# The layer-0 MLP's first product by one level of Strassen (seven half products for eight), with residual and gates resting in DRAM

## The chip, the core and the metric

The kernel runs on one core of a Trainium2 chip. A core has a matrix engine (TensorE, PE in the profile; PEld is its weight load), a vector engine (VectorE, DVE), a scalar engine (ScalarE, ACT), GpSimd (POOL) and SyncE (SP), which here issues the transfers between the chip's DRAM and the core's on-chip memory (SBUF). Each engine takes its own queue of instructions in order; they wait for each other by semaphores. TensorE adds its products up in PSUM, from where DVE or ACT must take them.

The metric is the device time of one execution in microseconds (us), as the median of several runs. Before the change it is 1242.63 us.

## The reference

Two layers of a diffusion transformer over 512 latent and 256 context tokens of width D = 1024. Layer 0 mixes tokens by pooling, layer 1 by attention. Each layer has a squared-ReLU MLP after its mixer, and each sub-layer is wrapped in RMS norms with shift, scale and gate that come from a linear map of the conditioning ("adaLN").

```
def sq_relu_mlp(h, w_in, w_out):
    return jnp.square(jax.nn.relu(h @ w_in)) @ w_out

for i in range(DEPTH):
    sh1, sc1, gt1, sh2, sc2, gt2 = ada_mods(c, w_ada[i], b_ada[i])
...
    x = x + gt1 * rms_norm(y_lat, g_mix_post[i])
    m_lat = sq_relu_mlp(modulate(rms_norm(x, g_mlp_pre[i]), sh2, sc2), w_mlp_in[i], w_mlp_out[i])
    x = x + gt2 * rms_norm(m_lat, g_mlp_post[i])
```

The context goes the same way through layer 0, with its own conditioning. `w_in` is 1024 x 4096, `w_out` 4096 x 1024, `w_ada` 1024 x 6144 per layer, all in float32.

## The kernel before

Precision: every float32 factor is split into a high part (a copy rounded to the matrix engine's fp32r form) and a low part (factor minus high), and each product is three matmuls: high by high, high by low, low by high. A weight block is thus loaded raw (1 MB, 128 partitions x 2048 columns) and split by a cast on ACT (L112) and a subtraction on DVE (L115), 2048 columns each. `Ring.load` does this: the raw block goes to one of three rotating buffers (pool `rawp`), the split halves to the next of three 4096-column units. The adaLN weights pass through the same three raw buffers.

The layer-0 MLP (`mlp`, from L580) works on all 768 tokens at once, in 16 groups of 256 hidden units. For a group:

- `w_out` of this group and `w_in` of the next are loaded and split into units.
- `Inner` (the class at L495) makes the first product of the next group: 2 blocks of 128 hidden units x 8 contraction blocks x 3 matmuls x 2 chunks of 384 tokens, 96 matmuls (L510) into PSUM. `square` takes them out: Relu (L518) and Square to the high part (L520) on ACT, r*r (L521) and its low part (L522) on DVE, 768 columns each.
- `out_mm` makes the second product of this group: 6 token tiles x 12 matmuls of 512 columns (L597), and `out_ev` adds each half tile to the running sum `acc` on DVE (L608), 12 additions of 128 x 512.

The first product of a group runs ahead of the second product of the one before it. Groups 14 and 15 are joined in one last second product.

DVE has a second task in the groups: `ada_sum` computes later adaLN vectors directly, without TensorE. For a 1 MB block of `w_ada` it makes one scaling (L238) and seven multiply-adds (L243) of 256 columns for each conditioning vector, a transpose (L246) and a reduction (L248). `extra0` starts one such block per group with two conditioning vectors (16 wide steps) while any are left and with one after that; `mid0` one with a single vector (8 steps). Their results are collected a group later (`ada_fin`, L211 and L221 in the profile). In group 6 `gate_diag` builds the MLP's gate rows.

Before the groups lies the prologue (the pool mixer, the first adaLN vectors on TensorE (L204), the norms, and the first product of group 0), whose steps have times written by hand (`Steps`). `residual` (L302) there updates the residual stream `xr` tile by tile. After the groups, `before0` and `last0` finish the last second product, add the residual, and start layer 1.

The order of instructions on each queue comes from a scheduler that simulates the program when it is built, except for those pinned by `keep_in_program_order` (the adaLN scalings, and all loads and splits up to group 1). Loads are issued from SyncE's queue (L98) in order; an issue waits until the last reader of the raw buffer that it takes is through.

Of the kernel before, what the change touches and what calls it, by code (L numbers as in the profile page):

```python
# [53 lines left out]
def backbone(ctx: ExitStack, tc, x, c, ctx_in, c_ctx, w_ada, b_ada, g_mix_pre, g_mix_post,  # L54
# [7 lines left out]
    rawp = ctx.enter_context(tc.tile_pool(name="rawp", bufs=3, side="right"))  # L62
    tmp = ctx.enter_context(tc.tile_pool(name="tmp", bufs=3, side="right"))
    psA = ctx.enter_context(tc.tile_pool(name="psA", bufs=2, space=PSUM))
    psB = ctx.enter_context(tc.tile_pool(name="psB", bufs=4, space=PSUM))

    xr = const.tile([P, NT, D], F32, name="xr")
    acc = const.tile([P, NT * D], F32, name="acc")
    gate = const.tile([P, 2, D], F32, name="gate")
    ident = const.tile([P, P], F32, name="ident")  # L70
# [6 lines left out]
    nhalf = const.tile([P, 4], F32, name="nhalf")  # L77
    junk = const.tile([P, D], BF16, name="junk")
# [3 lines left out]
    phase = ctx.enter_context(tc.tile_pool(name="phase", bufs=1)).tile([P, 40], F32, name="phase")  # L82
    rawe = ExitStack()
# [223 lines left out]

    def modulated_pair(t, i, s, hi, lo, works, wide, fine, on_act):
        ci = 0 if t < NL else 1
        sh = (SH1, SH2)[s] * KT  # L310
        sl = slice(t * P, (t + 2) * P)
        pss = []
# [12 lines left out]
        for q in range(4):  # L325
            h = works[q // 2][:, 512 * (q % 2):512 * (q % 2) + 512].rearrange("p (k n) -> p k n", n=256)
            for kk in range(2):
                k = 2 * q + kk
                sa, b = avec[i][s][:, k, ci:ci + 1], mods[i][:, sh + k, ci:ci + 1]
                if not on_act[k]:  # L330
                    ve.tensor_scalar(out=h[:, kk, :], in0=pss[q][:, kk, :], scalar1=sa, scalar2=b,
                                     op0=ALU.mult, op1=ALU.add)
                else:
                    sc.activation(h[:, kk, :], pss[q][:, kk, :], AF.Identity, scale=sa, bias=b)
            if fine:
                ks = slice(2 * q, 2 * q + 2)
                sc.copy(hi[:, ks, sl], h)  # L337
                ve.tensor_tensor(out=lo[:, ks, sl], in0=h, in1=hi[:, ks, sl], op=ALU.subtract)
            elif q % 2:
                ks = slice(2 * q - 2, 2 * q + 2)  # L340
                h = works[q // 2].rearrange("p (k n) -> p k n", n=256)
                sc.copy(hi[:, ks, sl], h)
                ve.tensor_tensor(out=lo[:, ks, sl], in0=h, in1=hi[:, ks, sl], op=ALU.subtract)

# [137 lines left out]
    def chunks0(g):  # L482
        if g == 0:
            return [[(1, 0, 512, 256)], [(0, 0, 0, 256)], [(0, 256, 256, 256)]], [(0, 1, 512, 0), (1, 1, 256, 512)]
        return [[(0, 0, 0, 384), (1, 0, 384, 384)]], [(0, 2, 384, 0)]
# [9 lines left out]
    class Inner:  # L495
# [6 lines left out]
        def part(self, c, f):  # L502
            (wH, wL), (aH, aL) = self.w, self.a
            if f not in self.ps:
                self.ps[f] = psA.tile([P, 2, 512], F32, tag="a", name="psin")
            ps, fs = self.ps[f], slice(f * P, (f + 1) * P)
            for k in range(KT):
                for n, (w, a) in enumerate(((wH, aH), (wH, aL), (wL, aH))):
                    for bank, o, t0, ln in self.chunks[c]:
                        te.matmul(ps[:, bank, o:o + ln], w[:, k, fs], a[:, k, t0:t0 + ln],  # L510
                                  start=(k == 0 and n == 0), stop=(k == KT - 1 and n == 2))

        def square(self, f):
            hi, lo = self.hid
            r = work_tile()[:, 0:self.ntok]
            q = work_tile()[:, 0:self.ntok]
            for b0, nb, ln, t0 in self.pieces:
                sc.activation(r[:, t0:t0 + nb * ln].rearrange("p (b n) -> p b n", n=ln),  # L518
                              self.ps[f][:, b0:b0 + nb, 0:ln], AF.Relu)
# [11 lines left out]

    ring = Ring(unit)

    def w_in(i, g, rg, pin=False, wait=None):
# [30 lines left out]
    for n, t in enumerate(order):  # L565
# [14 lines left out]
    def mlp(i, inner, rg, hids, order, extra, mid, last, before_last):  # L580
# [6 lines left out]
        def out_mm(parts, t, cols=HALVES):  # L587
            ts_ = slice(t * P, (t + 1) * P)
            pss = [psB.tile([P, 512], F32, tag="b", name="pso") for _ in cols]
# [19 lines left out]

        wo_, wi = w_out(i, 0, rg, True), w_in(i, 1, rg, True)  # L610
        for f in range(2):
            if len(inner.chunks) > 1:
                inner.part(len(inner.chunks) - 1, f)
            inner.square(f)
        for g in range(NG - 1):
            if g:
                wo_, wi = w_out(i, g, rg, g < 2), w_in(i, g + 1, rg, g < 2)
            part = (g, inner.hid, wo_)
            if g == NG - 2:
                wo_ = w_out(i, NG - 1, rg)  # L620
            extra(g)
            inner = Inner(g + 1, wi, aH, aL, hids[(g + 1) % len(hids)], CHUNKS[ntok], ntok)
            inner.run((lambda: mid(g)) if g < NG - 2 else None)
            if g < NG - 2:
                for t in range(tiles):
# [31 lines left out]
    def extra0(g):  # L657
# [7 lines left out]
        if g == 2:  # L665
            sc.activation(junk[:, 0:1], nhalf[:, 0:1], AF.Exp)
        if g == 6:
            gate_diag(0, GT2, 0)
            gate_diag(0, GT2, 1)

# [161 lines left out]

    def before0():
        qring.append(Ring([unit[0], unit[2], unit[1]]))
        w_chunk(2, 0, raw0)
# [7 lines left out]
    pTL = unit[1][:, 0:NT * LAT].rearrange("p (s n) -> p s n", n=LAT)  # L843
    pbuf = [xr[:, 4, 0:TOK], xr[:, 5, 0:TOK], gate[:, 1, 0:TOK], acc[:, 4 * D:4 * D + TOK]]
    aring = Ring([ra[:, 8192:12288], unit[0], unit[1], unit[2]])
# [16 lines left out]
    def s_scores(i):  # L862
# [5 lines left out]
        for n, (a, b) in enumerate(((qH, kTH), (qH, kTL), (qL, kTH))):  # L868
            for c2 in range(2):
# [4 lines left out]
        ve.tensor_reduce(out=sm[:, 0:1], in_=v, axis=AX.XY, op=ALU.max, negate=True)  # L874
        sc.activation(pbuf[i % 4].rearrange("p (c n) -> p c n", n=384), v, AF.Exp, bias=sm[:, 0:1],
                      accum_out=sm[:, 1:2])
        smx[i] = sm

    def s_norm(i):
        sm, p = smx[i], pbuf[i % 4]  # L880
        ve.reciprocal(sm[:, 2:3], sm[:, 1:2])
# [5 lines left out]
    def s_turn(i):  # L887
        _, t = steps[i]
        sl = slice(t * P, (t + 1) * P)
        p = pbuf[i % 4]  # L890
        for b in range(2):
# [171 lines left out]
```

## Time and profile before

| what | us |
|---|---|
| median of 3 runs (lowest, highest) | 1242.63 (1242.49, 1243.06) |
| the profiled execution, its own time | 1242.43 |
| its span, first to last instruction | 1240.4 |
| from the end of group 0's second product to the first product of group 15 | 446.43 |
| one group in it | 33.52 |

The profiled execution's time and its span differ by 2.0 us that lie around the instructions. The granted TensorE clock is 0.994 of full speed on average.

How its rows read: a row of grouped instructions gives line, engine, operation, output and inputs, shapes and a count, then the busy time in us, the mean in ns, and the idle time before it with what ended it. A row of the chain gives start and duration in us, then the engine and line that the end waited for. A row of the timeline gives start, busy time, engine, line and operation, with idle time in brackets. A row of windows gives the stretch, its length, then the busy time and count of PE, PEld, DVE, ACT and POOL, the granted clock, the busy share of the DMA engines and GB/s. A row of DMA issues gives the count, the size and the time from issue to landing. Where instructions follow each other without a gap, the step from start to start is shorter than the busy time of one, since the ends overlap; the steps are the price.

### The profile page before, as it was taken

The page shows a single profiled execution, that of the slowest core. Times are in us where ns is not written, and L with a number is a line of the kernel's source. Part 1 is how long each engine was busy: PE and PEld are TensorE (multiplying, and loading weights), DVE is VectorE, ACT ScalarE, POOL GpSimd, SP SyncE. Part 2 cuts the span into 40 slices and gives each one's busy share as a digit, 9 for nine tenths or more (in the row PEclk, how much of TensorE's full clock was granted, in tenths as well). Part 3 has the DMA queues.
Part 4 walks back from the last instruction along what each step waited for, and adds up shares of the span by engine and source line. Part 5 has one row for each costly group of instructions (what it writes and reads, how often), then busy time and mean ns, then how long its engine had stood idle before and what let it go on. Part 6 is the DMA issues. An engine that isn't in the chain of part 4 may idle for free.

```text
span 1240.4 us, 16687 instructions
## 1 busy us (share of the span) xinstructions
PE 1197.7 (97%) x6770; PEld 1043.0 (84%) x6770; DVE 868.1 (70%) x1424; ACT 452.5 (36%) x734; POOL 102.0 (8%) x135
## 2 busy tenths in 40 slices
PE   6799999999999999999999989999999999999997
PEld 5579889999888888899978869998878888888886
DVE  3788887788887877766387689972665564555555
ACT  5575122122212121222267357862633222313222
POOL 1061000000000000000152232001100000000001
PEclk9999999999999999999999999999999999999999
DMA  9991434444323344335121211011134232332201
GB/s 330 349 306 69 130 109 136 136 137 136 123 82 107 131 136 136 117 122 170 35 85 52 103 35 35 1 39 65 48 122 137 68 122 83 102 102 84 86 1 68
DMA packets 103276, 137.41 MB, mean 111 GB/s; under 512 B 2416, under 2 KB 87840, under 8 KB 103200
## 3 DMA queue, kind: packets, MB, share of 16 engines
q1 hardware_dynamic: 103200, 136.35, 33.8%
q8 instruction: 53, 0.87, 0.3%
q14 instruction: 23, 0.19, 0.0%
HBM read 134.24 MB, written 2.10 MB: 110 GB/s over the span
## 4 chain that ended last, share of the span: by engine, by line
PE 84%; DVE 5%; issue 3%; DMA 3%; ACT 3%; POOL 2%; SPq 0%; POOLq 0%; DVEq 0%; ACTq 0%
PE psin L510 35%; PE pso L597 34%; PE psy L935 3%; PE po L909 3%; PE psq L703 3%; PE pss L870 2%; PE pspool L442 2%; PE pspt L895 1%; DMA raw<-in_w_pool 1%; DMA raw<-in_w_ada 1%; ACT junk L138 1%; PE psada L204 1%; DVE xr L302 1%; DMA xr<-in_x 1%; DVE work L299 1%
## 5 line engine op out<-in xcount | busy, mean ns | idle before, releaser
L597 PE MATMUL pso<-units,rb 128*128 128x512 f32 (+1 forms) x1182 | 278.9, 391 | 1.7 <-DVE units L115 1.2
L608 DVE TENSOR_TENSOR acc<-acc,pso 128x512 f32<-128x512 f32 (+1 forms) x281 | 183.5, 680 | 125.5 <-PE pso L597 125.5
L597 PEld LDWEIGHTS pso<-units,rb 128*128 128x128 f32 x1182 | 220.5, 188 | 47.4 <-DVE units L115 1.6
L510 PE MATMUL psin<-ra,units 128*128 128x384 f32 (+1 forms) x1184 | 240.3, 345 | 0.9 <-ACT units L112 0.9
L510 PEld LDWEIGHTS psin<-ra,units 128*128 128x128 f32 x1184 | 209.1, 188 | 11.8 <-ACT units L112 1.7
L112 ACT CAST units<-raw 128x2048 fp32r<-128x2048 f32 (+1 forms) x50 | 80.1, 1623 | 263.4 <-PE pso L597 155.5
L243 DVE SCALAR_TENSOR_TENSOR rows<-raw,cond,rows 128x256 f32<-128x256 f32 x280 | 119.9, 478 | 0.2
L510 PE MATMUL psin<-ra,rb 128*128 128x384 f32 (+1 forms) x688 | 115.7, 320 | 2.8 <-ACT ra L337 1.6
L510 PEld LDWEIGHTS psin<-ra,rb 128*128 128x128 f32 x688 | 111.4, 189 | 4.2 <-ACT ra L337 2.0
L115 DVE TENSOR_TENSOR units<-raw,units 128x2048 fp32r<-128x2048 f32 (+1 forms) x48 | 95.3, 1998 | 24.8 <-ACT units L112 24.8
L518 ACT ACTIVATE work<-psin 128x512 f32<-128x512 f32 (+1 forms) x66 | 45.0, 685 | 178.2 <-PE psin L510 171.5
L521 DVE TENSOR_TENSOR work<-work 128x768 f32<-128x768 f32 (+1 forms) x64 | 52.6, 822 | 78.8 <-ACT work L518 78.5
L597 PE MATMUL pso<-ra,rb 128*128 128x512 f32 (+1 forms) x390 | 91.0, 386 | 0.0
L149 POOL TENSOR_SCALAR ms<-ss 128x1 f32<-128x1 f32 x21 | 8.8, 418 | 965.9 <-ACT junk L138 964.9
L597 PE MATMUL pso<-rb 128*128 128x512 f32 x360 | 85.3, 392 | 0.1
L597 PEld LDWEIGHTS pso<-ra,rb 128*128 128x128 f32 x390 | 72.5, 188 | 15.1 <-ACT rb L520 0.4
L510 PE MATMUL psin<-ra 128*128 128x512 f32 x256 | 80.2, 389 | 0.0
L597 PEld LDWEIGHTS pso<-rb 128*128 128x128 f32 x360 | 67.1, 188 | 13.8 <-DVE acc L606 0.4
L112 ACT CAST ra<-raw 128x2048 fp32r<-128x2048 f32 x16 | 30.4, 1908 | 105.4 <-PE pso L597 79.7
L510 PEld LDWEIGHTS psin<-ra 128*128 128x128 f32 x256 | 48.0, 188 | 10.0
L522 DVE TENSOR_TENSOR rb<-work,rb 128x768 fp32r<-128x768 f32 (+1 forms) x64 | 52.2, 815 | 3.0
L115 DVE TENSOR_TENSOR ra<-raw,ra 128x2048 fp32r<-128x2048 f32 x16 | 36.6, 2292 | 24.0 <-ACT ra L112 24.0
(174 smaller groups left out, 1582.9 us busy)
## 6 DMA issues: line engine op xcount, KB each, us to landing
raw<-in_w_ada SPq DMA_DIRECT2D x48, 1024.0 KB, 7.9
raw<-in_w_mlp_in SPq DMA_DIRECT2D x32, 1024.0 KB, 5.5
raw<-in_w_mlp_out SPq DMA_DIRECT2D x32, 1024.0 KB, 5.0
raw<-in_w_qkv SPq DMA_DIRECT2D x6, 1024.0 KB, 5.3
raw<-in_w_o SPq DMA_DIRECT2D x4, 1024.0 KB, 5.6
xr<-in_x SPq DMA_DIRECT2D x4, 512.0 KB, 4.7
out<-xr SPq DMA_DIRECT2D x8, 256.0 KB, 2.0
xr<-in_ctx SPq DMA_DIRECT2D x2, 512.0 KB, 5.6
```

What stands on the lines that cost most here:

```text
L112: a = gp.tensor_copy(hi, raw) if pool_hi else sc.copy(hi, raw)
L115: b = (gp if pool_lo else ve).tensor_tensor(out=lo, in0=raw, in1=hi, op=ALU.subtract)
L243: ve.scalar_tensor_tensor(out=r, in0=raw[:, k, :], scalar=cond[:, k, c:c + 1], in1=r, op0=ALU.mult, op1=ALU.add)
L510: te.matmul(ps[:, bank, o:o + ln], w[:, k, fs], a[:, k, t0:t0 + ln], start=(k == 0 and n == 0), stop=(k == KT - 1 and n == 2))
L518: sc.activation(r[:, t0:t0 + nb * ln].rearrange("p (b n) -> p b n", n=ln), self.ps[f][:, b0:b0 + nb, 0:ln], AF.Relu)
L521: ve.tensor_tensor(out=q, in0=r, in1=r, op=ALU.mult)
L522: ve.tensor_tensor(out=lo[:, f, :], in0=q, in1=hi[:, f, :], op=ALU.subtract)
L597: te.matmul(pss[h][:, 0:cols[h][1]], a[:, f, ts_], w[:, f, cols[h][0]:sum(cols[h])], start=(n == 0), stop=(n == len(seq) - 1))
L608: ve.tensor_tensor(out=d, in0=d, in1=ps[:, 0:w], op=ALU.add)
L703: te.matmul(ps, a[:, k, sl], w[:, k % 4, :], start=(k == 0 and n == 0), stop=(k == KT - 1 and n == 2))
L909: te.matmul(po[:, 0:256], v[:, kt, hs], p[:, kt, qs], start=(kt == 0 and n == 0), stop=(kt == NT - 1 and n == 2))
L935: te.matmul(ps, a[:, k, sl], w[:, k % 4, o:o + width], start=(k == 0 and n == 0), stop=(k == KT - 1 and n == 2))
```

## The change

In groups 2 to 15 of layer 0 the first product is one level of Strassen-Winograd: the activations (1024 x 768) are cut into four quarters (contraction halves by token halves of 384), the weights of a group (1024 x 256) into four quarters too, and seven products of half blocks replace eight. Each is 4 contraction blocks x 3 matmuls of 384 columns, 84 in all for 96. Sums of the products are formed in PSUM by letting a later product add to the bank of an earlier one, with copies of a bank between.

What comes with it:

- `sums()` builds the sums S1 to S4 of activation quarters and splits them, once, in group 1: 16 DVE additions of 384 columns, 8 ACT copies and 8 DVE subtractions of 768 columns.
- `weights_sums(g)` builds the weight sums T1 to T4 in each group and splits all seven operands: four DVE differences of 512 columns, two DVE lows of 1024, one of 1024 and one of 512 for T3, T4 and B22 (written into a quarter of the activations that is no longer read), with the ACT copies for the highs.
- `Seven.run` replaces `Inner.run`. Three copies of a PSUM bank on ACT, two DVE additions of 384 columns that read PSUM; then Relu, Square in place and the high copy on ACT, the low on DVE. r*r is no longer on DVE.
- Space: the sums take the place of `xr`, `gate` and `junk` and of unit 0. `w_in` operands take unit 1, and `w_out` has unit 2 alone. The three raw buffers stay three.
- `xr` is written to DRAM in the prologue, a 512 KB transfer per tile, at hand-written times, and read back in `before0`, which also makes the gate rows (`gate_diag`, in group 6 before).
- The tokens of the layer-0 MLP are stored in the order (t mod 2) * 3 + t div 2 of their tiles, so that the quarters lie together.

```diff
+        st.at([61.98, 66.18, 70.38, 74.58, 78.78, 82.98][n], lambda t: sy.dma_start(spill[:, t], xr[:, t]), t)
...
+        def put(n, j, a, b, op):
+            hs = slice(2 * HN * j, 2 * HN * j + 2 * HN)
...
+            for m in range(2):
+                ve.tensor_tensor(out=wide(w)[:, m], in0=a[:, m], in1=b[:, m], op=op)
+            hi, lo = (h3[:, hs], l3[j]) if n == 3 else (z[:, hs] for z in at[n])
+            sc.copy(hi, w)
+            ve.tensor_tensor(out=lo, in0=w, in1=hi, op=ALU.subtract)
...
+        for j in range(2):
+            a11, a21, a12, a22 = (src[:, u, h, 2 * j:2 * j + 2] for u in range(2) for h in range(2))
+            w1 = put(1, j, a21, a22, ALU.add)
+            w2 = put(2, j, w1, a11, ALU.subtract)
+            put(4, j, a12, w2, ALU.subtract)
+            put(3, j, a11, a21, ALU.subtract)
+
+    def weights_sums(g):
+        raw = raw_load(w_mlp_in[0, :, g * 256:(g + 1) * 256].rearrange("(k p) n -> p k n", p=P), 256)
...
+        B11, B21 = put(unit[1][:, 0:2048], rv[:, 0], 1024)
+        tt = work_tile()
+        t1, t2 = k4(tt[:, 0:512]), k4(tt[:, 512:1024])
+        ve.tensor_tensor(out=t1, in0=b12, in1=b11, op=ALU.subtract)
+        ve.tensor_tensor(out=t2, in0=b22, in1=t1, op=ALU.subtract)
+        T1, T2 = put(unit[1][:, 2048:4096], k4(tt), 1024)
+        tu = work_tile()
+        ve.tensor_tensor(out=k4(tu[:, 0:512]), in0=b22, in1=b12, op=ALU.subtract)
+        ve.tensor_tensor(out=k4(tu[:, 512:1024]), in0=b21, in1=t2, op=ALU.subtract)
...
+        T3, T4 = put3(0, 2, tu.rearrange("p (m k n) -> p m k n", m=2, n=P))
+        B22, = put3(2, 1, b22.unsqueeze(1))
+        return [(B11, A11), (T1, S[1]), (T2, S[2]), (B21, A12), (T3, S[3]), (B22, S[4]), (T4, A22)]
...
+        def run(self, between=None):
+            px, py = (psA.tile([P, 2, 512], F32, tag="a", name="psin") for _ in range(2))
+            a, b, c, e = px[:, 0, 0:HN], px[:, 1, 0:HN], py[:, 0, 0:HN], py[:, 1, 0:HN]
+            r0, r1 = (work_tile()[:, 0:TOK] for _ in range(2))
+            self.chain(a, 0, True, False)
+            sc.copy(b, a)
+            self.chain(e, 1, True, True)
+            sc.copy(r1[:, 0:HN], e)
+            self.chain(a, 2, False, False)
+            sc.copy(c, a)
+            self.chain(b, 3, False, True)
+            sc.activation(r0[:, 0:HN], b, AF.Relu)
+            self.chain(a, 4, False, False)
+            ve.tensor_tensor(out=r1[:, HN:TOK], in0=r1[:, 0:HN], in1=a, op=ALU.add)
+            self.chain(c, 5, False, True)
+            ve.tensor_tensor(out=r1[:, 0:HN], in0=r1[:, 0:HN], in1=c, op=ALU.add)
+            if between:
+                between()
+            self.chain(a, 6, False, True)
+            sc.activation(r0[:, HN:TOK], a, AF.Relu)
+            sc.activation(r1, r1, AF.Relu)
+            hi, lo = self.hid
+            for f, r in enumerate((r0, r1)):
+                sc.activation(r, r, AF.Square)
+                sc.copy(hi[:, f, :], r)
+                ve.tensor_tensor(out=lo[:, f, :], in0=r, in1=hi[:, f, :], op=ALU.subtract)
...
         for g in range(NG - 1):
-            if g:
+            if i == 0:
+                if g:
+                    wo_, products = w_out(i, g, one(unit[2])), weights_sums(g + 1)
+            elif g:
                 wo_, wi = w_out(i, g, rg, g < 2), w_in(i, g + 1, rg, g < 2)
...
-        if g == 6:
-            gate_diag(0, GT2, 0)
-            gate_diag(0, GT2, 1)
...
     def before0():
+        nonlocal xr, gate, junk
+        S["held"].close()
+        xr, gate, junk = residents(ctx)
+        gate_diag(0, GT2, 0)
+        gate_diag(0, GT2, 1)
+        for t in (4, 5, 0, 1, 2, 3):
+            sy.dma_start(xr[:, t], spill[:, t])
```

More of the change, by code (lines that the diff above doesn't have):

```diff
@@ new lines, in backbone, with __init__, chain @@
+    class Seven:
+        def __init__(self, products, hid):
+            self.products = products
+            self.a, self.ntok = (hH, hL), TOK
+            self.hid = [z.rearrange("p (f n) -> p f n", n=TOK) for z in hid]
+        def chain(self, bank, n, start, stop):
+            (wH, wL), (aH, aL) = self.products[n]
+            for k in range(4):
+                for m, (w, a) in enumerate(((wH, aH), (wH, aL), (wL, aH))):
+                    te.matmul(bank, w[k], a[k], start=start and k == 0 and m == 0, stop=stop and k == 3 and m == 2,
+                              skip_group_check=True)
+        def run(self, between=None):
[24 more added lines that the diff above has]
+                ve.tensor_tensor(out=lo[:, f, :], in0=r, in1=hi[:, f, :], op=ALU.subtract)
@@ L608, in out_ev @@
                     ve.tensor_tensor(out=d, in0=d, in1=ps[:, 0:w], op=ALU.add)
[L610 to L612 removed]
+        if i == 0:
+            one = lambda z: Ring([z])
+            wi = w_in(i, 1, one(unit[1]))
+            for f in range(2):
                 inner.part(len(inner.chunks) - 1, f)
[L614 removed]
+                inner.square(f)
+            wo_ = w_out(i, 0, one(unit[2]))
+            sums()
+        else:
+            wo_, wi = w_out(i, 0, rg, True), w_in(i, 1, rg, True)
+            for f in range(2):
+                if len(inner.chunks) > 1:
+                    inner.part(len(inner.chunks) - 1, f)
+                inner.square(f)
         for g in range(NG - 1):
[L616 removed]
+            if i == 0:
+                if g:
+                    wo_, products = w_out(i, g, one(unit[2])), weights_sums(g + 1)
+            elif g:
                 wo_, wi = w_out(i, g, rg, g < 2), w_in(i, g + 1, rg, g < 2)
             part = (g, inner.hid, wo_)
[L619 removed]
+            if g == NG - 2 and i:
                 wo_ = w_out(i, NG - 1, rg)
             extra(g)
[L622 removed]
+            if i == 0 and g:
+                inner = Seven(products, hids[(g + 1) % len(hids)])
+            else:
+                inner = Inner(g + 1, wi, aH, aL, hids[(g + 1) % len(hids)], CHUNKS[ntok], ntok)
             inner.run((lambda: mid(g)) if g < NG - 2 else None)
+            if g == NG - 2 and i == 0:
+                wo_ = w_out(i, NG - 1, one(unit[1]))
             if g < NG - 2:
```

89 lines of the change are left out of this document (72 added, 17 removed).

## The prediction

> **What bounds the kernel now.** I read the page first: busy shares, then the chain that ended last, then the chain inside one layer-0 MLP group, then sums over that stage, then single instructions.
>
> ```profile
> PE 1197.7 (97%) x6770; PEld 1043.0 (84%) x6770; DVE 868.1 (70%) x1424; ACT 452.5 (36%) x734; POOL 102.0 (8%) x135
> PE 84%; DVE 5%; issue 3%; DMA 3%; ACT 3%; POOL 2%; SPq 0%; POOLq 0%; DVEq 0%; ACTq 0%
> ```
>
> TensorE sets the end: 97% busy, 84% of the chain. Around the change it is complete. One group, from the chain (start, duration, what):
>
> ```profile
> 213.98 5.66 PE pso L597 x24
> 219.65 1.41 PE psin L510 x8
> 221.06 1.39 PE pso L597 x6
> 222.45 15.26 PE psin L510 x88
> 237.71 9.56 PE pso L597 x42
> ```
>
> 96 first-product matmuls of 384 columns and 72 second-product ones of 512, no gap: one takes 15.26/88 = 0.1734 us and 9.56/42 = 0.2276 us. The next group starts 33.52 us later. The stage in windows (length, then PE, PEld, DVE, ACT, POOL busy, clock, DMA share, GB/s):
>
> ```profile
> 145.35:591.78 446.43, 444.93 (x2441) 400.56 (x2442) 355.68 (x644) 98.55 (x84) 0.00 (x0) 1.00 0.40 128
> 213.98:247.50 33.52, 33.52 (x186) 30.32 (x185) 26.82 (x50) 7.14 (x7) 0.00 (x0) 1.00 0.39 126
> 314.34:351.48 37.14, 36.47 (x209) 31.94 (x209) 28.85 (x53) 9.39 (x11) 0.00 (x0) 1.00 0.36 114
> 519.08:552.60 33.52, 33.52 (x185) 30.32 (x185) 23.45 (x41) 7.14 (x7) 0.00 (x0) 1.00 0.39 126
> ```
>
> PE has no idle time, yet VectorE (DVE) has only 33.52 - 26.82 = 6.7 us of it per group. The third row is the group with gate_diag, 3.6 us longer. The last is a group that carries one-column adaLN sums only. The question is whether 6.7 us of slack pays for what the change gives DVE.
>
> **The change, part by part.**
>
> *Seven products (groups 2 to 15).* 84 matmuls for 96: 12 x 0.1734 = 2.08 us of PE per group, 14 x 2.08 = 29.1 us. PE's floor per group is 33.52 - 2.08 = 31.44 us.
>
> *DVE work per group.* Steps between starts give the prices (start, busy):
>
> ```profile
> 224.07 2.46 DVE L243 SCALAR_TENSOR_TENSOR rows<-raw,cond,rows 128x256 f32<-128x256 f32 x6
> 226.44 2.28 DVE L115 TENSOR_TENSOR rb<-raw,rb 128x2048 fp32r<-128x2048 f32 x1
> 228.65 2.06 DVE L243 SCALAR_TENSOR_TENSOR rows<-raw,cond,rows 128x256 f32<-128x256 f32 x5
> 230.96 0.96 DVE L521 TENSOR_TENSOR work<-work 128x768 f32<-128x768 f32 x1 [0.25 <-ACT work L518]
> 231.84 0.48 DVE L243 SCALAR_TENSOR_TENSOR rows<-raw,cond,rows 128x256 f32<-128x256 f32 x1
> 239.46 0.68 DVE L608 TENSOR_TENSOR acc<-acc,pso 128x512 f32<-128x512 f32 x1
> 240.06 0.95 DVE L522 TENSOR_TENSOR rb<-work,rb 128x768 fp32r<-128x768 f32 x1
> ```
>
> 2048 columns: 228.65 - 226.44 = 2.21 us. 768: 0.88. 512: 0.60. One adaLN step: 2.37/6 = 0.395. Per column about 1.08 ns, so for sizes without a row I estimate 384 at 0.47 and 1024 at 1.13. Removed: one weight split (2.21) and two r*r (0.88 each, now ScalarE), 3.97 us. Added: four 512-wide differences (2.40), two 1024-wide lows (2.26), the 512 and 1024 lows of the last three weight sums (1.73), two PSUM adds of 384 (0.94), 7.33 us. Net +3.36: DVE's group becomes 26.82 + 3.36 = 30.2 us. That is 1.3 us under PE's floor: on busy time alone the change would win. An access to PSUM or to the strided quarter could cost DVE 0 to 30% more than the flat rows (L608 reads PSUM at 0.60, as flat ones do), +-0.8 us; I take 0. ScalarE, by two groups of the whole run (busy, mean ns):
>
> ```profile
> L112 ACT CAST units<-raw 128x2048 fp32r<-128x2048 f32 x39 | 74.1, 1906 | 263.4 <-PE pso L597 155.5 <-DMA raw<-in_w_mlp_out 63.5 <-PE psin L510 24.4
> L520 ACT ACTIVATE rb<-work 128x768 fp32r<-128x768 f32 x32 | 27.2, 849 | 1.0
> ```
>
> A 2048 cast leaves (-1.9); copies to the seven weight operands' highs (3072 columns in four pieces, some 3.6), three PSUM copies of 384 (some 1.5), smaller Relu pieces (+0.2) and two copies of 768 (1.7) come: about 12.3 us for 7.14. It is not the bound.
>
> *Where the transfers go.* This decides, I think. The raw ring has three 1 MB buffers and each group makes four loads through it (w_out, w_in, two-column adaLN, one-column adaLN), before and after. Landing times and issue times before:
>
> ```profile
> raw<-in_w_ada SPq DMA_DIRECT2D x22, 1024.0 KB, 5.9
> raw<-in_w_mlp_out SPq DMA_DIRECT2D x13, 1024.0 KB, 5.0
> raw<-in_w_mlp_in SPq DMA_DIRECT2D x12, 1024.0 KB, 5.5
> ...
> 219.41 0.37 SPq L98 DMA_DIRECT2D raw<-in_w_mlp_out  x1
> 228.75 0.37 SPq L98 DMA_DIRECT2D raw<-in_w_mlp_in  x1
> 234.79 0.99 SPq L98 DMA_DIRECT2D raw<-in_w_ada  x2
> ```
>
> Both adaLN loads go out at 234.79 and are first needed at the next group (from 248): 13 us for a 5.9 us landing. That works because w_out is split into a free unit in mid-group (226.44 above), which frees its raw buffer early. After the change w_out has a single unit, in use until the previous second product ends. So its split (cast, then subtraction) comes at the group's start, and its raw buffer is held until then. The built kernel's order then puts the one-column adaLN load into exactly that buffer: SyncE issues it only after the w_out subtraction. In DVE's queue, behind that subtraction, stand one 1024-wide low (1.13) and about two adaLN steps (0.8), and then the first instruction that needs that load. DVE takes its queue in order: 5.5 us of landing less 1.95 us of work is a stall of 3.6 us, in which evictions, PSUM adds and weight sums behind it all wait. The same happens a second time: w_in takes the buffer of the two-column sum, issued after that sum's reduction, and DVE reaches the first weight difference 3.2 to 4.2 us later: a stall of 1.3 to 2.3, say 1.8.
>
> The Trainium skill ("DMA: Bandwidth & Descriptors", Anatomy of one DMA — SWDGE (gpsimd) path) fits a transfer as 2.0 us plus bytes over 436 GB/s, 4.4 us for 1 MB; the rows here say 5.0 to 5.9. By 4.4 both stalls would shrink by 1.1 us, and the sum below by about 26 us, to 1240; the rows are this kernel's own transfers, so they stand.
>
> Sum over 13 windows between w_out subtractions (groups 1 to 14):
> - DVE work 13 x 30.2 = 392.6. The first also carries the rest of sums() (+6.5: 16 additions and 8 lows, part of them before the window), two with one-column work lack 3.4 each (26.82 - 23.45): 392.
> - Stalls: ten mixed windows 10 x about 4.9 = 49 (5.4 less where an eviction fills the gap). The two one-column windows 7.4 and 9.3 (half the adaLN steps, so less cover). The first 9.4 (its w_in load waits for sums). 75 us.
> - 467 against 446.4 (first window row, from the first group's product to the first product of group 15). Seven of group 15 starts some 4 us before the last of these subtractions: +17 us. PE's saving of 29 us is inside this: PE waits for DVE, so nothing of it is seen but in group 15, which ends the stage.
> Bounds: a landing of 5.0 to 5.9 us (the rows above) for 5.5 moves some 25 stalls by -0.5 to +0.4 each, -12 to +10; DVE work +-2%, +-8.
>
> *Spills in the prologue.* Six 512 KB stores of xr enter SyncE's queue between the adaLN loads:
>
> ```profile
> 60.00:70.00 10.00, 10.00 (x113) 7.66 (x111) 8.04 (x17) 5.45 (x12) 1.92 (x4) 1.00 1.10 348
> 90.00:100.00 10.00, 8.79 (x74) 8.44 (x72) 9.75 (x16) 9.07 (x18) 6.36 (x7) 1.00 0.01 2
> ...
> 58.67 17.53 SPq L98 DMA_DIRECT2D raw<-in_w_ada  x5
> ...
> 68.48 2.46 DVE L302 SCALAR_TENSOR_TENSOR xr<-acc,rs,xr 128x1024 f32<-128x1024 f32 x2
> ...
> 83.00 1.00 PE psada L204 x16
> ...
> 94.68 3.61 PE psin L510 x28
> ...
> 145.37 1.91 ACT units L112
> ```
>
> The transfers are saturated at 348 GB/s to 90 us and empty after. The first spill needs the xr that DVE finishes at about 69.7; SyncE waits there with loads behind it, which before were issued between 58.67 and 76.2. What was in flight (about three loads) drains at some 67.4, so 2 to 3 us are lost. From 70 on, five loads and the three spills among them are 6.8 MB, at 0.348 MB/us 19.6 us: the last adaLN load lands near 90 to 91, against 76.2 + about 6 = 82 before. PE used the last of these loads from 83.00 (chain row) and began the first product at 94.68; some of that distance is normalisation that doesn't need the loads, so of 8 to 9 us not all comes through. The other three spills stand before w_out(0) and w_in(1), which have 10 us of slack and more. I take +6 us, bounds +2 (mostly hidden by that distance) and +9 (all of it).
>
> *The rest.* The reload of xr (3 MB) is issued during Seven of group 15, behind over 10 us of PE work: 0. gate_diag moves from the 3.6 us hiccup, already part of the 446.4, to the end: its 8 matmuls and small waits +0.5 (bounds 0 and 3.6). The permuted token order and the PSUM accumulation across chains change no count: 0, bounds +-2, as layer 1 is rescheduled.
>
> Sum: 1242.4 + 6 + 17 + 0.5 = 1266 us. The profiled execution took 1242.43 us (span 1240.4), 0.2 under the median 1242.63; I make no correction.
>
> **The rivals.**
> (1) *The loads arrive in time and PE stays the bound.* For it: the busy sum, 30.2 < 31.44, and a DMA share of 0.39. Against it: issue times tied to the w_out split. Time: -29.1 for PE, -1.8 for gate_diag's hiccup against its end, +6 prologue, +10 in the first Seven group (sums() and the cold weight pipeline on DVE: 16 x 0.47 + 8 x 0.88 = 14.6 us, mostly bare): about 1228.
> (2) *Half the stall is filled.* Evictions stand between the stalled instructions and so PE is fed: group near 33.4 us, gain and loss cancel: 1242.
> (3) *Worse than forecast.* The landings lengthen, as in the prologue (7.9 median over the whole kernel):
>
> ```profile
> raw<-in_w_ada SPq DMA_DIRECT2D x48, 1024.0 KB, 7.9
> ```
>
> Each us more on 25 stalls is 25 us: 1291. Against it: the stage's DMA share 0.39, so loads hardly meet. The Trainium skill ("TensorE: Matmul & The Clock Gate", Why this matters for your kernels) warns that PE idle for more than about 3 us falls back to half clock; here the gaps I foresee are 1 to 3 us but for a few, and the clock column of every row above is 1.00, so no run here shows it. A half-clock spell of 3.4 us per stall pair would cost 12 x 1.7 = 20 us, 1286, the same place.
> The other side of my forecast is (1); its point of decision: the one-column load must land within about 2 us of DVE's need, that is a group under 33.2 us.
>
> **How the numbers follow.** Forecast 0.62; (1) 0.19; (2) 0.07; (3) 0.12. Time 1266. The likeliest's own range: 1252 to 1282 (landing, work and prologue together). The range 1228 to 1288 leaves out half of (1) and half of (3) and a little more. Faster by over 0.2% (2.5 us, about what this measurement can tell from none): (1) and a third of (2), 0.21. Within: 0.05, from (2). Slower: 0.74.
>
> **What would show it.** Right: DVE idle before the first adaLN scaling on the one-column load, released by that transfer, about 3.5 us in each group from 2 on; a second one before the first weight difference, 1 to 2 us; PE gaps ended by DVE; groups of 34 to 36 us; the last prologue adaLN transfer near 91 us, the end of the first group's product at 151 or so (145.37 before). Wrong: groups at 31.5 us with PE gapless (1); a PE clock below 1.00 in the stage, or loads of 7 us (3); a DVE busy time well over 31 us per group would put the loss on work, not on waits; a prologue unchanged to 1 us would take away its +6.

## The result, and the profile after

The changed kernel takes 1250.45 us (median of 4 runs, 1249.18 to 1253.27) against 1242.85 for the kernel before: the ratio is 1.0061, 95% interval 1.0041 to 1.0081. It is slower, by 7.6 us, inside the range and on the side that was forecast, but by a third of the 23 us that were forecast. The profiled execution took 1250.13 us (span 1248.2).

The page of the changed kernel: busy time, the granted clock in 40 slices, the chain by engine.

```profile
PE 1191.6 (95%) x6602; PEld 1017.9 (82%) x6602; DVE 923.5 (74%) x1546; ACT 524.6 (42%) x868; POOL 101.8 (8%) x135
PEclk9899989999999999999999989999999999999999
PE 78%; DVE 9%; DMA 6%; ACT 3%; issue 1%; POOL 1%; SPq 1%; DVEq 0%; POOLq 0%; ACTq 0%
```

TensorE's busy time fell by only 6 us, though 168 matmuls of 0.1734 us (29.1 us) are gone. So either it does other work or the same matmuls take longer. Most of the groups of the changed stage, in one window (length, then PE, PEld, DVE, ACT, POOL, clock, DMA share, GB/s):

```profile
200.00:540.00 340.00, 338.82 (x1797) 296.08 (x1796) 316.06 (x604) 121.31 (x155) 0.00 (x0) 1.00 0.41 130
```

PE is idle for 1.2 us of 340: it is still nearly the whole bound, not DVE. SyncE's issues (start, duration) give the length of a group and the places of the loads; the first and last row are w_out loads eleven groups apart:

```profile
205.30 0.37 SPq L106 DMA_DIRECT2D raw<-in_w_mlp_out  x1
...
382.30 10.80 SPq L106 DMA_DIRECT2D raw<-in_w_ada  x2
398.69 0.37 SPq L106 DMA_DIRECT2D raw<-in_w_mlp_out  x1
414.42 0.37 SPq L106 DMA_DIRECT2D raw<-in_w_mlp_in  x1
...
558.84 0.37 SPq L106 DMA_DIRECT2D raw<-in_w_mlp_out  x1
```

A group takes (558.84 - 205.30)/11 = 32.14 us, 1.38 less than before. The forecast had some 35. The pair of adaLN loads spreads from 382.30 to 393.10: the second, with one column, goes out at about 392.7. What it waited for, and what DVE then does (start, duration):

```profile
391.97 0.69 DVE L615 TENSOR_TENSOR work<-raw,work 128x512 f32<-128x512 f32 x1
...
396.37 2.29 DVE L123 TENSOR_TENSOR units<-raw,units 128x2048 fp32r<-128x2048 f32 x1
...
400.64 0.35 DVE L246 TENSOR_SCALAR rows<-raw,cond 128x256 f32<-128x256 f32 x1
```

L615 is the last reader of w_in's raw block, L123 the w_out subtraction, L246 the first use of the one-column block. The load leaves when L615 is done, before L123, and is needed 8 us after its issue. It takes w_in's buffer. The next w_out leaves at 398.69, as L123 ends: w_out's buffer goes to the next w_out. That is not the assignment on which the forecast stood. DVE's waits for loads from 185 to 580 (total, times, longest):

```profile
DVE work L610 <- DMA raw<-in_w_mlp_in: 8.4, 6, 2.6
```

Of the loads it waits for w_in alone, as forecast for the second stall, but only six times in these twelve groups: 8.4 us in all, where 75 were forecast for both.

If the groups are shorter than before, where do the 7.6 us come from? TensorE at the end of group 0 and the start of group 1 (idle time before it in brackets), and the windows there:

```profile
136.86 16.95 PE L731 MATMUL pso<-units,rb 128*128 128x512 f32 x72
161.68 0.61 PE L219 MATMUL psada<-part,sel 128*32 128x4 f32 x16 [7.87 <-DVE part L256]
162.22 6.67 PE L731 MATMUL pso<-units,rb 128*128 128x512 f32 x18
```

```profile
160.00:165.00 5.00, 3.28 (x23) 2.60 (x24) 3.42 (x11) 1.31 (x2) 0.00 (x0) 0.50 0.97 314
165.00:170.00 5.00, 5.00 (x19) 4.02 (x18) 5.00 (x9) 2.35 (x3) 0.00 (x0) 0.79 1.05 312
```

Three things are to be read. Group 0's second product ends at 153.8 where it ended at 145.4 before: 8.4 us lost in the prologue. Then PE is idle for 7.9 us, until DVE ends a reduction. And then 18 matmuls of 512 take 6.67 us, 0.37 each: the granted clock is 0.50 after the gap. A fourth loss is in the price of the matmul itself. Groups of 512-column matmuls over the whole run (busy, mean ns), and the chain in layer 1 (start, duration), whose code was not changed:

```profile
L731 PE MATMUL pso<-units,rb 128*128 128x512 f32 x1530 | 374.8, 397 | 1.9 <-DVE units L123 1.7
```

```profile
1008.93 5.46 PE pso L731 x24
...
1020.80 5.59 PE pso L731 x24
...
1030.95 5.60 PE pso L731 x24
...
1042.91 5.44 PE pso L731 x24
```

In the kernel before, the same group had a mean of 392 ns, and each 24 of layer 1 took 5.44:

```profile
L597 PE MATMUL pso<-units,rb 128*128 128x512 f32 x1170 | 277.1, 392 | 1.7 <-DVE units L115 1.2 <-ACT gate L294 0.4
```

```profile
1004.10 5.44 PE pso L597 x24
...
1015.89 5.44 PE pso L597 x24
```

Half of layer 1's runs of 24 now take 5.59, 0.233 us a matmul for 0.2267. In layer 0 nearly all do (in the chain, 36 take 8.39).

The two profiles also show where the time is lost on balance. The layer-0 MLP's last product ends at 640.8 us, 0.9 earlier than before (641.7): what the groups save has paid for the prologue and the gap. Layer 1's MLP, whose code was not changed, takes 362 us from its first matmul to its last for 356 before.

### The profile page after: what moved, and what is told of

It is laid out like the page before. It is cut to its first block, busy times and chain, and to the rows that moved or that the text cites. A ratio compares the mean times of both kernels' runs of the same rounds, so it can differ in the third digit from the quotient of the medians.

```text
span 1248.2 us, 16629 instructions
## 1 busy us (share of the span) xinstructions
PE 1191.6 (95%) x6602; PEld 1017.9 (82%) x6602; DVE 923.5 (74%) x1546; ACT 524.6 (42%) x868; POOL 101.8 (8%) x135
## 4 chain that ended last, share of the span: by engine, by line
PE 78%; DVE 9%; DMA 6%; ACT 3%; issue 1%; POOL 1%; SPq 1%; DVEq 0%; POOLq 0%; ACTq 0%
PE pso L731 30%; PE psin L636 16%; PE psin L526 14%; PE psq L851 5%; DMA raw<-in_w_ada 4%; PE psy L1090 3%; PE po L1064 3%; PE pss L1025 2%; DMA raw<-in_w_mlp_in 2%; PE pspt L1050 1%; ACT junk L146 1%; PE pspool L454 1%; DVE xr L310 1%; PE psada L212 1%; DVE units L123 1%
## 5 line engine op out<-in xcount | busy, mean ns | idle before, releaser
L731 PE MATMUL pso<-units,rb 128*128 128x512 f32 x1542 | 376.6, 396 | 1.9 <-DVE units L123 1.7
L731 PEld LDWEIGHTS pso<-units,rb 128*128 128x128 f32 x1542 | 289.2, 189 | 66.4 <-DVE units L123 2.0
L123 DVE TENSOR_TENSOR units<-raw,units 128x2048 fp32r<-128x2048 f32 (+1 forms) x44 | 86.2, 1972 | 28.1 <-ACT units L120 28.1
L731 PE MATMUL pso<-ra,rb 128*128 128x512 f32 (+1 forms) x390 | 91.1, 386 | 0.0
L526 PE MATMUL psin<-ra,units 128*128 128x512 f32 (+1 forms) x320 | 87.5, 375 | 0.0
L731 PEld LDWEIGHTS pso<-ra,rb 128*128 128x128 f32 x390 | 72.6, 188 | 15.2
L636 PE MATMUL psin<-ra,units 128*128 128x384 f32 x336 | 66.2, 342 | 1.2 <-ACT psin L648 0.6
L526 PEld LDWEIGHTS psin<-ra,units 128*128 128x128 f32 x320 | 58.7, 188 | 9.3
L636 PE MATMUL psin<-sums,units 128*128 128x384 f32 x336 | 65.4, 342 | 0.5 <-ACT psin L644 0.3
L636 PEld LDWEIGHTS psin<-ra,units 128*128 128x128 f32 x336 | 58.0, 188 | 4.7 <-ACT psin L648 3.2
L636 PEld LDWEIGHTS psin<-sums,units 128*128 128x128 f32 x336 | 57.7, 188 | 3.0 <-ACT psin L644 1.8
L123 DVE TENSOR_TENSOR ra<-raw,ra 128x2048 fp32r<-128x2048 f32 x16 | 36.6, 2291 | 25.2 <-ACT ra L120 25.2
L851 PE MATMUL psq<-units,ra 128*128 128x512 f32 x216 | 53.0, 397 | 0.0
L659 ACT ACTIVATE work<-work 128x768 f32<-128x768 f32 x14 | 11.9, 847 | 91.5 <-DVE work L654 91.5
L526 PE MATMUL psin<-rb,ra 128*128 128x512 f32 x128 | 49.9, 390 | 0.0
```

The source lines that it names most:

```text
L123: b = (gp if pool_lo else ve).tensor_tensor(out=lo, in0=raw, in1=hi, op=ALU.subtract)
L526: te.matmul(ps[:, bank, o:o + ln], w[:, k, fs], rhs, start=(k == 0 and n == 0), stop=(k == KT - 1 and n == 2))
L636: te.matmul(bank, w[k], a[k], start=start and k == 0 and m == 0, stop=stop and k == 3 and m == 2, skip_group_check=True)
L731: te.matmul(pss[h][:, 0:cols[h][1]], a[:, f, ts_], w[:, f, cols[h][0]:sum(cols[h])], start=(n == 0), stop=(n == len(seq) - 1))
L851: te.matmul(ps, a[:, k, sl], w[:, k % 4, :], start=(k == 0 and n == 0), stop=(k == KT - 1 and n == 2))
```

## The experiments

All medians of a set stand against the kernel before on the same chip (1242.8 to 1243.5), and against 1250.45 for the changed kernel, which was not run again in the sets; a difference of 1 us from it says nothing.

### Where the weight units lie: e1 and e2

The change also set the spacer ahead of the units from 40 to 24 floats. By the built programs' addresses the units begin 160 bytes past a multiple of 256 in the kernel before and 96 past one in the changed kernel; the other matmul operands, ra and rb, stay at 160 in both.

```diff
-    phase = ctx.enter_context(tc.tile_pool(name="phase", bufs=1)).tile([P, 24], F32, name="phase")
+    phase = ctx.enter_context(tc.tile_pool(name="phase", bufs=1)).tile([P, 40], F32, name="phase")
```

> The changed kernel with one number altered: the spacer tile ahead of the weight units is 40 floats again, as in the kernel before, so that the units lie 64 bytes higher (160 past a multiple of 256 bytes as before, instead of 96). Theory (address): 512-column matmuls took 0.2332 us in the changed kernel against 0.2276 before, and in unchanged code of layer 1 every second run of 24 took 5.59 us against 5.44, because their streamed operand lies in the units at another offset. Then L731 x24 is 5.44 to 5.46 again everywhere and the time falls by 72 x 0.0056 x 16 = 6.5 us in layer 0 and by some 3.5 in layer 1: about 1240.5. Rival (contention): the matmuls are slowed by what DVE, ACT and the transfers do in the same memory, or by the whole layout; then nothing changes, 1249 to 1252.

> The kernel before with the spacer at 24 floats: the units lie 64 bytes lower and nothing else differs. Theory (address): second-product matmuls whose weights lie in the two units behind the spacer go from 0.2276 to about 0.233 us, those whose weights lie in the third unit (another tile) stay; +4 to +9 us, 1247 to 1252. Rival (contention or layout): 1242 to 1244.

Measured: e1 1243.88 us (ratio to before 1.0009, 0.9999 to 1.0020), 6.6 less than the changed kernel; e2 1249.94 (1.0064, 1.0039 to 1.0089), 7.1 more than before. The group of L731 in e1, and layer 1's chain in e2:

```profile
L731 PE MATMUL pso<-units,rb 128*128 128x512 f32 x1530 | 369.6, 394 | 1.9 <-DVE units L123 1.7
```

```profile
1018.58 5.59 PE pso L597 x24
...
1040.69 5.44 PE pso L597 x24
```

The old kernel gets the slow runs from nothing but the 64 bytes, and the new one loses them. The address theory holds; contention is out, since e2 does no other work. In e2 layer 1's MLP takes 360 us, which would make the offset 4 of the 6 us lost there. e1's profile has 360 too, but with a clock of 0.74 to 0.92 in four windows of 5 us between 885 and 930, so this division is rough. The gain of e1 is smaller than the 10 us expected (1240.5): its groups go from 32.14 to only 31.94 us, where 0.40 was to be had. The chains of both kernels run through w_in's load at some 315 and 381 us, so the rest may go into that wait; this is argued, not shown. Why the offset matters, no run tells.

### The six stores of xr: e3 and e4

e3 takes the line with the stores out of the prologue's steps and puts them behind the first MLP loads:

```diff
-        st.at([61.98, 66.18, 70.38, 74.58, 78.78, 82.98][n], lambda t: sy.dma_start(spill[:, t], xr[:, t]), t)
...
             wo_ = w_out(i, 0, one(unit[2]))
+            for t in (4, 5, 0, 1, 2, 3):
+                tc.keep_in_program_order(sy.dma_start(spill[:, t], xr[:, t]))
             sums()
```

e4 adds the removed line to the kernel before.

> The changed kernel with the six stores of xr moved in SyncE's queue behind the prologue's adaLN loads and the loads of w_in(1) and w_out(0), pinned there; the same work. Theory (the stores delay the loads): the last prologue adaLN load lands near 82 to 83, as before, and group 0's second product ends 5 to 8 us earlier than in the changed kernel (153.7); the time falls by as much, to 1243 to 1246, unless DVE, which is busy without a break from 119 to 161, keeps part of it: then group 1's product starts 3 us earlier or less and the time is 1247 or more. Rival (the prologue's delay comes from the other edits there, permuted tokens and the spaced layout): no change, 1250.

> The kernel before with the six stores of xr added at the changed kernel's places in the queue, and nothing read back. Theory: the prologue lengthens by what it did in the changed kernel, the end of group 0's second product goes from 145.4 to 151 to 154, and all of it is kept, as PE has no idle time behind: 1249 to 1251. Rival: the stores are hidden, 1242 to 1244.

Measured: e3 1243.68 (1.0004, 0.9993 to 1.0015), 6.8 less than the changed kernel; e4 1248.35 (1.0048, 1.0032 to 1.0064), 5.5 more than before. In e3, group 0's second product starts 5.5 us earlier than in the changed kernel (136.86), but the gap behind it stays:

```profile
131.36 16.95 PE L730 MATMUL pso<-units,rb 128*128 128x512 f32 x72
156.18 0.61 PE L219 MATMUL psada<-part,sel 128*32 128x4 f32 x16 [7.87 <-DVE part L256]
```

So the stores cost 5.5 us in the kernel before, and in the changed kernel 6.8 more where they were than behind the loads. What they still cost there is open, as no run of the changed kernel leaves them out. Group 0's second product still ends 3.0 us later in e3 than before (148.3 for 145.4), and no run tells why. The gap is another matter.

### The shared buffer: e5

The forecast's premise made true: the one-column block can only go into w_out's raw buffer.

```diff
-    def raw_load(src, width, pool=None):
-        t = (pool or pools[0]).tile([P, 2048], F32, tag="raw", name="raw")
+    def raw_load(src, width, pool=None, tag="raw"):
+        p = pool or pools[0]
+        kw = dict(bufs=1 if tag == "rawh" else 2) if p is rawp else {}
+        t = p.tile([P, 2048], F32, tag=tag, name="raw", **kw)
...
-                       .rearrange("(k p) n -> p k n", p=P), 256).rearrange("p (k n) -> p k n", n=256)
+                       .rearrange("(k p) n -> p k n", p=P), 256, None, "rawh" if nc_ == 1 else "raw").rearrange("p (k n) -> p k n", n=256)
...
-        return rg.load(w_mlp_out[i, g * 256:(g + 1) * 256, :].rearrange("(k p) n -> p k n", p=P), D, pin)
+        return rg.load(w_mlp_out[i, g * 256:(g + 1) * 256, :].rearrange("(k p) n -> p k n", p=P), D, pin, tag="rawh")
```

> The changed kernel with the three raw buffers given out by hand: w_out and the one-column adaLN block share one, w_in has one of its own with the prologue's, the two-column block the third. This makes the prediction's premise true: the one-column load can only go out behind w_out's split. The prediction's step would have each group stall 3.6 us for it, groups of 34 to 35.5 us, the time 1270 to 1290. Theory: a late load is moved behind other DVE work by the scheduler that orders the queue, and the waits that are left in the changed kernel are those for w_in (0.7 to 2.6 us, every second group), which has now its own buffer; then groups of 31.7 to 32.0 us for 32.1 and 1245 to 1250.

Measured: 1274.37 (1.0248, 1.0232 to 1.0264), 24 us more than the changed kernel. That is the size that the forecast had, yet it lies elsewhere. DVE's waits from 185 to 580, then from 530 to 640:

```profile
DVE units L125 <- ACT units L122: 5.6, 2, 4.2
...
DVE rows L248 <- DMA raw<-in_w_ada: 1.2, 2, 0.9
```

```profile
DVE units L125 <- ACT units L122: 16.6, 4, 7.0
...
DVE rows L248 <- DMA raw<-in_w_ada: 5.8, 2, 3.4
```

By the w_out issues, the eight mixed groups (with both kinds of adaLN block) from 266.52 to 529.98 take 32.9 us each, not 34 to 35.5: DVE waits 1.2 us for adaLN blocks from 185 to 580, as the built order puts other work in front. The loss is in two early groups (37.6 and 38.7 us) and the last two (42.7 and 38.2), which have half the adaLN steps to stand in front, and there it is mostly w_out's cast that DVE waits for. At the end the edit does more than make the premise true. It leaves w_out a single buffer, so the last w_out load goes out only behind the split of the one before it (the changed kernel had issued both by 569.79):

```profile
620.90 2.30 DVE units L125
623.22 5.06 DMA raw<-in_w_mlp_out
628.30 1.91 ACT units L122
```

Both expectations fell: the forecast's in how the cost is spread, and the theory's 1245 to 1250 altogether. This assignment of the buffers costs 24 us, of which the forecast's stall is only a part; the changed kernel avoids it.

### The gap in group 1: e6

```diff
-        ada_step(0, dual or lone)
+        ada_step(0, [] if g == 0 else dual or lone)
...
     def before0():
...
+        ada_step(0, [])
```

> The changed kernel with no two-column adaLN block in group 0; all later blocks move up one place and the last one-column block falls into group 14 (same work in all). Theory: in group 1 TensorE stands still for 7.9 us because DVE has sums(), evictions and 16 adaLN steps before w_out(1)'s split, and then runs at half clock until about 167 us; without the block's 7.6 us the gap falls under 2 us, and with it the half clock (another 2 us): 1241 to 1244. Rival (w_out(1)'s load or unit 2 sets the start, not DVE's work): the gap stays near 8 us, 1249 to 1251.

Measured: 1243.37 (1.0003, 0.9992 to 1.0014), 7.1 less than the changed kernel. TensorE, and one of the windows where the changed kernel had 0.50:

```profile
153.72 2.96 PE L731 MATMUL pso<-units,rb 128*128 128x512 f32 x12
156.53 3.63 PE L636 MATMUL psin<-sums,units 128*128 128x384 f32 x20
160.76 2.35 PE L636 MATMUL psin<-ra,units 128*128 128x384 f32 x12 [0.61 <-ACT psin L648]
```

```profile
160.00:165.00 5.00, 4.39 (x25) 4.24 (x25) 5.00 (x12) 0.96 (x2) 0.00 (x0) 1.00 0.57 184
```

The gap and the half clock behind it are gone. But the edit takes away two things, the block's steps on DVE and its load through the raw buffers. In the built program of the changed kernel w_in(2) takes w_out(1)'s raw buffer; in e6 it takes w_out(0)'s, which is free early. So its load goes out at 158.10 in the changed kernel and at 109.75 in e6:

```profile
153.85 1.90 ACT L120 CAST units<-raw 128x2048 fp32r<-128x2048 f32 x1 [13.99 <-PE pso L731]
158.10 0.37 SPq L106 DMA_DIRECT2D raw<-in_w_mlp_in  x1
```

```profile
109.75 0.37 SPq L106 DMA_DIRECT2D raw<-in_w_mlp_in  x1
142.54 2.25 PE L636 MATMUL psin<-ra,units 128*128 128x384 f32 x12
```

w_out has one unit, so the split of w_out(1) begins only when group 0's second product ends (153.8). In e6 TensorE has half products of group 2 (L636) to do beside that split; in the changed kernel it has none, as w_in(2) is not there. DVE's block then adds the time from 158.1, the end of the split, to 161.7. How the gap divides between the late load and DVE's work, no run tells.

### The QKV low: e7

```diff
-            st.at(5.5, lambda: split(*raw0[0], True, False, True))
+            st.at(5.5, lambda: split(*raw0[0], True, False, False))
```

> The changed kernel with the first QKV chunk's low part made on DVE instead of GpSimd. Between the MLP's last product and the first large QKV products the changed kernel needs 63.1 us for 59.4 before. Theory: GpSimd's 5.17 us subtraction stood before the norms' small GpSimd steps, because its unit comes free only with the last half product; on DVE it takes 2.2 us beside other work: 2 to 4 us less, 1246 to 1248. Rival (the reload of xr or the gate rows set the pace there): 1249 to 1251.

Measured: 1248.36 (1.0042, 1.0029 to 1.0056). It lands in the expected range but not by the expected cause: from the last chain piece of the MLP's product to the first 34 QKV products the profile still has 64.3 us (609.46 to 673.78). The theory fell: layer 1's MLP begins at 879 us with and without the edit, so what e7 is faster by lies behind that. The 63 and 59 us of its expectation also start from unlike points, as the kernel before has 24 of the last product's 144 matmuls done ahead; counted to the end of that product (before 641.7, changed 640.8) the two kernels differ by 0.9 us there.

### Together: e8 and e9

e8 holds the edits of e1, e3, e6 and e7, e9 those of e1, e3 and e6.

> Spacer of 40 floats, late stores, no block in group 0 and the QKV low on DVE together, same result. Theory: the four effects lie in different stretches and add up: 1250.5 - 6.6 - 6.8 - 7 - 3 = 1227, below both kernels. Rival (each removal only uncovers the next wait, as DVE is at 30 us of 32 in each group): 1234 to 1240.

> Spacer of 40 floats, late stores and no block in group 0 together; the QKV low stays on GpSimd as in the changed kernel. Theory (the place of that subtraction is without effect, as alone it made 1248.4 with a transition no shorter): 1231 to 1235, as with it. Rival (it is worth 2 us): 1235 to 1237.

Measured: e8 1233.13 (0.9918, 0.9904 to 0.9933), e9 1233.22 (0.9922, 0.9907 to 0.9937). Both beat the kernel before, with all the work done. The three single gains would add up to 20.5 (1230.0); 17.2 came. e8 lies just under the rival's 1234 to 1240 and far from the theory's 1227. The place of the QKV low has no effect that these two medians show. DVE's waits in e9 from 200 to 540 show what was uncovered:

```profile
DVE work L610 <- DMA raw<-in_w_mlp_in: 13.1, 7, 3.6
```

### What w_in's wait is worth: e10 and e11

e10 is e9 with `lone = []` (no one-column adaLN blocks) and constants for the vectors that are then not computed. e11 is e9 with the order of two calls changed:

```diff
-                    wo_, products = w_out(i, g, one(unit[2])), weights_sums(g + 1)
+                    products = weights_sums(g + 1)
+                    wo_ = w_out(i, g, one(unit[2]))
```

> The same three edits, and the sixteen one-column adaLN blocks left out: layer 1's vectors of those kinds are a constant 0.5 instead. Three loads per group for three raw buffers, and 3.9 us less DVE work. Theory (what keeps groups at 32.3 us is DVE's wait for w_in, whose buffer comes free only with an adaLN reduction, 15.2 us in seven waits): the wait goes and groups fall to PE's floor, 31.4 to 31.6 us: 1220 to 1224. Rival (the floor is higher, as chains wait for PSUM copies and adds between them): groups of 32 us or more, 1229 or more.

> The three edits, and in each group w_in's load asked for ahead of w_out's, full result: w_in then takes the buffer that w_out's split frees at the group's start, 20 us before it is needed, and w_out the one that w_in's sums free, some 5 us before its split is needed. Theory: the wait for w_in goes, a shorter one for w_out may come: groups of 31.5 to 32.0 us, 1222 to 1229. Rival (w_out lands too late, TensorE waits for its split): groups of 33 us or more, 1240 or more.

Measured: e10 1220.76 (0.9824, 0.9806 to 0.9842), e11 1229.27 (0.9900, 0.9882 to 0.9919). SyncE's issues in e10, then the window of e11:

```profile
370.67 0.37 SPq L106 DMA_DIRECT2D raw<-in_w_mlp_out  x1
...
402.20 0.37 SPq L106 DMA_DIRECT2D raw<-in_w_mlp_out  x1
433.75 0.37 SPq L106 DMA_DIRECT2D raw<-in_w_mlp_out  x1
```

```profile
200.00:540.00 340.00, 339.80 (x1823) 302.19 (x1822) 318.10 (x602) 128.77 (x160) 0.00 (x0) 1.00 0.40 130
```

With three loads for three buffers a group takes 31.53 us, PE's floor (31.44 by the forecast's arithmetic). e10 leaves out DVE work as well as loads, so it shows the floor and not the wait alone. e11 keeps all the work: PE is idle for 0.2 us of 340 (3.2 in e9), DVE has no wait for w_in left, and its groups take 31.8 us by the w_out issues. It is the fastest that does all the work, 13.5 us under the kernel before, at the upper end of what was expected.

## Why the prediction was wrong in size

- *PE's floor and DVE's work.* Right. 31.44 us forecast, 31.53 in e10; DVE 30.2 us per group forecast, 316.06/340 x 32.14 = 29.9 measured. The unknown sizes came out at the estimates: a PSUM add of 384 at 0.48 (DVE's step from L652 at 380.19 to 380.67), a low of 1024 at 1.13 (365.00 to 366.13).
- *"The built kernel's order then puts the one-column adaLN load into exactly that buffer."* This step failed. I had taken the three raw buffers to be handed out in turn, from the order of issues and what each waits for, and had not looked at which buffer each load is given. In the built program w_out keeps one buffer and the other three loads alternate over two. In the kernel before they are not handed out in turn either: w_in and w_out share one, and each adaLN load has its own, so the early split of w_out was not what let those loads out. In the changed kernel the one-column load leaves 8 us before its need, and some 45 us of the forecast stalls (3.6 in each group and more in the one-column ones) didn't exist.
- *The price of that stall.* Wrong in its form too. In e5, where the premise is made true, mixed groups lose 0.8 us each and not 3.6: the built order puts other work in front of a late load. The rest of the 24 us falls in the first groups and the last, in part by w_out's single buffer.
- *w_in's stall, 1.8 us in each group.* The mechanism is there (L610, 0.3 to 2.6 us), the count was off: half of the groups. It matters more once others are gone, 13.1 us in e9, and e11 removes it.
- *The prologue, +6 us.* Right in mechanism and place, a little low: the last adaLN pieces run at 92.13 (91 forecast), group 0's product ends 8.4 us later; the stores alone are worth 5.5 (e4) to 6.8 (e3). SyncE's wait for xr is the term that was too small: from 65 to 70 us the transfers carry 41 GB/s for 348 before, 4.4 us lost where 2 to 3 were forecast.
- *Group 1.* sums() was in the sum as DVE time. The gap of PE beside it, 7.9 us, was not in the sum; taking out group 0's block wins 7.1 us (e6). Here, and not where the forecast had it, a load stands behind w_out's split: that of w_in(2).
- *Order and place of data, "0, bounds +-2".* Failed: 64 bytes in the units' place are worth 6.6 us in this kernel (e1). I counted instructions and left the addresses out.
- *The clock, "no run here shows it".* True of the rows shown there; elsewhere the kernel before had it too (0.51 from 740 to 745 us, behind a gap of 3.41). After PE's 7.9 us gap the window's clock is 0.50. The Trainium skill ("TensorE: Matmul & The Clock Gate", Part 1: The HAM clock gate) has half clock after some 3.4 us without work and full clock again after as long at work. The trace is near it for the fall: by windows of 1 us the clock is 0.93 from 156 to 157 and 0.50 from then on, 3.1 us after PE's last matmul. The return took longer: with PE at work from 161.7 the clock is 0.50 to 167 and 0.95 from 167 to 168. The rival put half clock in every group; among the groups, it came at the one long gap.

So the forecast had the side right in part by luck. Its 75 us of stalls were 8.4 us of waits, and terms that it had at nothing or too small made the kernel slower: stores, group 1 and addresses. With all three taken out (e9) the other terms leave a gain of 9.5 us. Rival (1) was right that PE stays the bound in the groups. That its 1228 lies near e9 (1233) and e11 (1229) is luck as well: it holds +6 for the prologue and +10 for sums(), most of which these runs have taken out, and without them it would say 1212.

## To carry to other kernels

- Before a stall is priced, read from the built program which buffer each load is given and who reads that buffer last; the order of issues doesn't tell it. Here the busy sum under the floor (30.2 against 31.4) was the better guide.
- When an edit moves tiles in memory, treat their addresses as part of the change, and try the old offset first: one number was worth as much as the transfers.
- A one-time piece of work (sums(), 15 us of DVE) costs what is queued beside it in its group, on the engine and through the buffers. Move optional work and its loads out of that group, and stores behind the loads that the next product needs.

## What was not expected of the hardware

512-column matmuls whose streamed weights begin 96 bytes past a multiple of 256 took 0.233 us, those at 160 bytes 0.2267 to 0.228, with the same work and code and, in the groups, a clock of 1.00 (e1, e2). The 384-column ones of the first product stream the activations, which lie at 160 bytes in both kernels, so they are no test of it. Two offsets were tried; what lies between them is open.
